# Trunk kernel on one core: block products of the feed-forward parts in strict order on TensorE, six matmuls per bank

## The chip, the cores and the metric

The kernel runs on one core of one Trainium2 chip. The metric is device time in microseconds, the median of several runs. Before the change it is 2380.13 us (3 runs, 2378.37 to 2385.53). All details below come from one profiled execution of that kernel, which took 2382.98 us. Engine names are those of the profile: PE is TensorE, PEld its weight loads, DVE VectorE, ACT ScalarE, POOL GpSimd, SP SyncE, which issues the transfers.

## The reference, cut to what matters

Two layers; each is a half-step feed-forward part, a mixing part, and another half-step feed-forward part. Sequence 512, model width 1024, hidden width 2816, everything in float32:

```python
def _swiglu(t, w_gate, w_up, w_down):
    return (jax.nn.silu(t @ w_gate) * (t @ w_up)) @ w_down
...
for l in range(DEPTH):
    f = _swiglu(_rmsnorm(h, ffn1_pre_g[l]), ffn1_w_gate[l], ffn1_w_up[l], ffn1_w_down[l])
    h = h + 0.5 * _rmsnorm(f, ffn1_post_g[l])
    ...  # three attention branches, gated, summed, projected
    f = _swiglu(_rmsnorm(h, ffn2_pre_g[l]), ffn2_w_gate[l], ffn2_w_up[l], ffn2_w_down[l])
    h = h + 0.5 * _rmsnorm(f, ffn2_post_g[l])
```

The change concerns the four feed-forward parts only. The kernel and the profile call them a0, c0 (layer 0), a1 and c1 (layer 1).

## The kernel before, in words

**A float32 product.** Each operand is split into a high part and a low part that TensorE takes at full rate. The split (`split`, L179) is one ScalarE copy for the high part (`wh`, L182) and one VectorE subtraction for the low part (`wl`, L183). One product of a 128-row tile is then three matmuls into the same PSUM bank, `mm3`: high by high (L205), high by low (L206), low by high (L207).

**Seven products for eight.** In a feed-forward part, most of the hidden width goes through a scheme of Strassen's kind: of a 2 by 2 product of blocks, seven block products are made instead of eight, of sums and differences of blocks. They are numbered 0 to 6 and run in the order 0, 2, 1, 3, 4, 5, 6. There are two column groups (0 and 1), and for each one a *gate* group and an *up* group of seven products (`token_product`, names `pw...g` and `pw...u`), then the *down* products of both (`product`, names `pd...`). Names carry the part: `pwc0g` is a gate product of c0, `pda` a down product of part a.

One product uses two PSUM banks, `pts[0]` and `pts[1]` (the loop variable `e`). Its weights come in two units of two 128-row tiles each (`k0` is 0 and 2, `kk` runs from 0 to 3). So it has 24 matmuls of 512 columns, 12 for each unit. Several products add into the same banks: products 0 and 2 open a pair, a copy of the first pair opens the third, and the table `SUM` says which product adds where. Product 6 uses the banks of product 5 and adds to the sum that stands in them; that sum has a use of its own and is read first. In the token groups that read is a VectorE addition, L777, one for each bank.

**Weights.** A unit's weights are loaded by SP (L297 for a block, 512 KB), combined with another block where the product needs that (VectorE, L327), and split (L182, L183). `wh` and `wl` are rings of four units. `Queue` (L350) emits a job's units, then those of the next jobs (four units ahead, `load_ahead`), and then the job's matmuls.

**Between the up group and the down products** the hidden values must be turned from one layout into the other. `turn`, called at two points of each unit, takes a finished part of the hidden values through a ScalarE copy (L800), a transpose by a transfer on SP (L801), and a ScalarE copy back (L804). The down products' first factors (`first_factor`) are made from these, with names `ah...` and `al...`.

**What sets the order.** The program emits instructions in the order of the jobs: all seven products of gate 0, of up 0, of gate 1, six of up 1, the first factor of the first down product, the last of up 1, and then the down products with plain gate and up tiles between them. A scheduler then orders the instructions of each engine by its own model; it may put a matmul that is ready by this model ahead of one that is emitted earlier. `tc.keep_in_program_order` ties an instruction to the one that stands before it on its engine in program order, so that the scheduler can't let it move. In the kernel before, the products' matmuls carry no such tie.

The loops that the change touches are those of `token_product` (from L740) and `product` (from L851), and `mm3` (L203).

Of the kernel before, what the change touches and what calls it, by code (L numbers as in the profile page):

```python
# [18 lines left out]
P = 128  # L19
# [4 lines left out]
def kernel(  # L24
# [38 lines left out]
    nc = tc.nc  # L63
# [4 lines left out]
    ND = D // P  # L68
# [7 lines left out]
    FC = 8  # L76
# [22 lines left out]
    def tmp(name):  # L99
        return sb.tile([P, S], F32, tag="f32t", bufs=5, name=name)  # L100
# [3 lines left out]
    def stile(shape, tag, name, dt=F32R):  # L104
        return sb.tile(shape, dt, tag=tag, bufs=BUFS[tag], name=name)
# [4 lines left out]
    def pbank(tag, name):  # L110
        return ps.tile([P, S], F32, tag=tag, bufs=4, name=name)
# [88 lines left out]
        nc.vector.scalar_tensor_tensor(t, z, minus, t, ALU.max, ALU.add)  # L200
        nc.scalar.activation(t, t, AF.Exp, scale=-1.0, bias=minus)

    def mm3(pt, lh, ll, rh, rl, start, stop, free=False):  # L203

        nc.tensor.matmul(pt, lh, rh, start=start, stop=False, skip_group_check=free)  # L205
        nc.tensor.matmul(pt, lh, rl, start=False, stop=False, skip_group_check=free)  # L206
        nc.tensor.matmul(pt, ll, rh, start=False, stop=stop, skip_group_check=free)  # L207

# [394 lines left out]
    def ffn(l, src, wg, wu, wd, dst, name, spare, parked, plan, aside=None):  # L603
# [12 lines left out]
        def hidden_rows(i):  # L616
            if i not in hr:
                hr[i] = stile([P, FC // 2, S], ("k", "tri")[i // 2], f"hr{name}_{i}", F32)
            return hr[i]
# [114 lines left out]
        def in_product(n):  # L734
            if n in (0, 1, 6):
                i, j = ((0, 0), (0, 1), None, None, None, None, (1, 1))[n]
                return [block(i, j, part) for part in range(2)]
            return st["u", n]

        def token_product(ci, up, n, uns):  # L740

            nm = f"{name}{'gu'[up]}_{ci}_{n}"
            if n in (0, 1, 2):
                st["c", n] = [pbank("z" if n == 0 else "mm", f"pw{nm}_{e}") for e in range(2)]
            if n == 1:
                for e in range(2):
                    nc.scalar.copy(st["c", 1][e][:], st["c", 0][e][:])
            if n == 0:
                if not up:
                    st["s", ci] = {}  # L750
            pts = st["c", SUM[n]]
            h, l = in_product(n)
            opens, ends = n in (0, 2), n in (1, 4, 6)
            for un in uns:
                for k in range(un.nk):
                    kk = un.k0 + k
                    for e in range(2):
                        c = slice(e * P, (e + 1) * P)
                        mm3(pts[e][:], h[:, kk, c], l[:, kk, c], un.h[:, k], un.l[:, k], opens and kk == 0,
                            ends and kk == ND // 2 - 1, free=True)  # L760
                        yield 3 * S * PE_US
                    turn(kk)
            if n == 0:
                return
            q = TO[n]
            g = st["s", ci]
            if not up and q not in g:
                g[q] = stile([P, FC // 2, S // 2], "f", f"s{name}_{ci}_{q[0]}{q[1]}", F32)[:]
            g = g[q]
            r = hidden_rows(2 * ci + q[1])[:, :, HALVES[q[0]]] if up else g  # L770
            for e in range(2):
                p = pts[e][:].rearrange("p (f q) -> p f q", f=2)
                re, ge = r[:, 2 * e:2 * e + 2], g[:, 2 * e:2 * e + 2]
                if n in (2, 3):
                    nc.scalar.copy(re, p)
                elif n in (4, 5):
                    nc.vector.tensor_tensor(re, re, p, ALU.add)  # L777
                elif up:
                    nc.vector.tensor_tensor(ge, p, ge, ALU.mult)
                else:  # L780
                    nc.scalar.activation(re, p, AF.Silu)
            if n in (4, 5):
                if up:
                    nc.vector.tensor_tensor(g, r, g, ALU.mult)
                else:
                    nc.scalar.activation(r, r, AF.Silu)
            if up and n in (1, 4, 5, 6):
                turns.append([nm, g, (2 * ci + q[1], q[0]), n in (1, 5), 0, None])

        def turn(kk):  # L790

            for one in turns:
                nm, g, (row, i), own, age, planes = one
                if kk == 1 and age == 0:
                    one[5] = planes = ([stile([P, 2, 2 * S], "rs", "tr" + nm, U16)[:, h] for h in range(2)] if own else
                                       [tmp(f"tr{nm}_{h}")[:].bitcast(U16) for h in range(2)])
                    words = g.rearrange("p f q -> p (f q)").bitcast(U16)
                    for h, plane in enumerate(planes):
                        part = tmp(f"th{nm}_{h}")[:].bitcast(U16)
                        nc.scalar.copy(part, words[:, h::2])  # L800
                        nc.sync.dma_start_transpose(plane.rearrange("p (r q) -> p r q", q=P), part)  # L801
                if kk in (0, 1) and age == 2:
                    r = hidden_rows(row)[:].bitcast(U16)
                    nc.scalar.copy(r[:, :, i * S + kk:(i + 1) * S:2].rearrange("p f (e q) -> p e f q", e=2),  # L804
                                   planes[kk].rearrange("p (e f q) -> p e f q", e=2, q=P))
                if kk == ND // 2 - 1:
                    one[4] += 1
            turns[:] = [one for one in turns if one[4] < 3]
# [20 lines left out]
        def first_factor(ci, n):  # L829

            a = lambda i, j: hr[2 * ci + j][:, :, HALVES[i]]
            nm = f"{name}_{ci}_{n}"
            h, l = (stile([P, FC // 2, S // 2], "v", f"a{x}{nm}")[:] for x in "hl")
            if n == 2:
                st["s", ci] = stile([P, FC // 2, S // 2], "v", f"as{nm}", F32)[:]
            s = st.get(("s", ci))
            if n == 2:
                nc.vector.tensor_tensor(s, a(1, 0), a(1, 1), ALU.add)
            elif n == 3:
                nc.vector.tensor_tensor(s, s, a(0, 0), ALU.subtract)  # L840
            elif n == 4:
                nc.vector.tensor_tensor(s, a(0, 1), s, ALU.subtract)
            elif n == 5:
                nc.vector.tensor_tensor(s, a(0, 0), a(1, 0), ALU.subtract)
            src = (a(0, 0), a(0, 1), s, s, s, s, a(1, 1))[n]
            split(h, l, src)
            st["a", ci, n] = h, l
# [3 lines left out]
        def product(at, uns):  # L851
            ci, n = DOWN[at]
            first, last = ci == 0, ci == NC - 1
            if at == 0:
                RINGS["o"] = 2
                dst.begin()
            if at + 1 < len(DOWN):
                first_factor(*DOWN[at + 1])
            if first and n in (0, 2):
                st["b", SUM[n]] = [pbank("z", f"pd{name}_{n}_{e}") for e in range(2)]  # L860
            pts = st["b", SUM[n]]
            h, l = st.pop(("a", ci, n))
            opens, ends = first and n in (0, 2), last and n in (1, 4, 6)
            for un in uns:
                for k in range(un.nk):
                    kk = un.k0 + k
                    for e in range(2):
                        c = slice(e * P, (e + 1) * P)
                        mm3(pts[e][:], h[:, kk, c], l[:, kk, c], un.h[:, k], un.l[:, k], opens and kk == 0,
                            ends and kk == FC // 2 - 1, free=True)  # L870
                        yield 3 * S * PE_US
                    turn(kk)
            if not last:
                return
            if n == 0:
                st["b", 1] = [pbank("z", f"pd{name}_1_{e}") for e in range(2)]
                for e in range(2):
                    nc.scalar.copy(st["b", 1][e][:], pts[e][:])
                return
            i, hf = TO[n]  # L880
            for e in range(2):
                f = dst.fs[2 * i + e][:, HF[hf]]
                if n in (4, 5):
                    nc.vector.tensor_tensor(f, f, pts[e][:], ALU.add)
                else:
                    nc.scalar.copy(f, pts[e][:])
# [817 lines left out]
```

## Time and profile before

| | us |
|---|---|
| median of 3 runs | 2380.13 |
| lowest, highest | 2378.37, 2385.53 |
| the profiled execution | 2382.98 |
| its span in the trace | 2380.9 |
| TensorE busy, matmuls | 2350.6 (11719) |
| VectorE busy | 1803.5 (2358 instructions) |
| ScalarE busy | 1513.8 (2306 instructions) |

The span is the time from the first to the last instruction in the trace; 2.1 us of the execution lie around it. A matmul in the profile shows about 0.39 us because matmuls are pipelined, while their starts show the pace. A row of a timeline has start, duration, engine, line, operation, the tile written and the tiles read (buffer numbers left out); in brackets stands how long the engine was idle ahead of it and what ended that. A row of a table of windows has the window, its length, busy time and number of instructions of PE, PEld, DVE, ACT and POOL, then the granted TensorE clock as a share of the full one, the share of time that the transfer engines were busy, and GB/s.

### The profile page before, as it was taken

How to read it: one execution, taken by the hardware profiler on the slowest of the kernel's cores; microseconds unless marked ns; L12 is line 12 of the kernel's file. 1: busy time of each engine (PE TensorE's matmuls, PEld its weight loads, DVE VectorE, ACT ScalarE, POOL GpSimd, SP SyncE). 2: the span in 40 equal slices, each digit the busy share in tenths (PEclk: the TensorE clock that was granted, in tenths of full speed). 3: DMA queues.
4: the chain of work that ended last, by engine and by line, in shares of the span. 5: the costliest groups of instructions: out<-in, count | busy, mean ns of one | idle time of the engine just before them, and what ended most of it. 6: DMA issues, size and time to landing. Idle time of an engine off the chain costs nothing.

```text
span 2380.9 us, 31151 instructions
## 1 busy us (share of the span) xinstructions
PE 2350.6 (99%) x11719; PEld 1984.2 (83%) x11719; DVE 1803.5 (76%) x2358; ACT 1513.8 (64%) x2306; POOL 75.8 (3%) x134
## 2 busy tenths in 40 slices
PE   9999999999999999999999999999999999999998
PEld 7787889888888888778888878889888888888787
DVE  8886877667777689778788778766767767888785
ACT  6777465577766556775656665655777665567744
POOL 0000000000111000000000000000001100000000
PEclk9999999999999999999999999999999999999999
DMA  5666455223223556664647664542323235566643
GB/s 197 195 174 174 161 196 151 71 80 94 87 78 103 189 179 182 170 195 135 236 128 200 186 185 153 192 124 71 94 76 98 73 123 193 161 204 174 197 143 141
DMA packets 299754, 354.98 MB, mean 149 GB/s; under 512 B 78266, under 2 KB 192978, under 8 KB 299604
## 3 DMA queue, kind: packets, MB, share of 16 engines
q1 hardware_dynamic: 299508, 352.97, 48.0%
q8 instruction: 92, 1.51, 0.3%
q14 instruction: 58, 0.48, 0.1%
q0 software_dynamic: 96, 0.03, 0.0%
HBM read 319.39 MB, written 16.78 MB: 141 GB/s over the span
## 4 chain that ended last, share of the span: by engine, by line
PE 85%; DVE 5%; DMA 4%; ACT 4%; issue 2%; SPq 0%; DVEq 0%; ACTq 0%
PE pg L206 4%; PE pg L205 4%; PE pg L207 4%; PE pdc L206 3%; PE pdc L207 3%; PE pdc L205 3%; PE pda L206 2%; PE pda L207 2%; PE pda L205 2%; PE pb L207 2%; PE pb L206 2%; PE pb L205 2%; PE pq L206 1%; PE pq L205 1%; PE pk L207 1%
## 5 line engine op out<-in xcount | busy, mean ns | idle before, releaser
L205 PE MATMUL pg<-us_a,wh_wg 128*128 128x512 f32 x384 | 151.0, 393 | 0.0
L207 PE MATMUL pg<-us_a,wl_wg 128*128 128x512 f32 x384 | 149.8, 390 | 0.0
L206 PE MATMUL pg<-us_a,wh_wg 128*128 128x512 f32 x384 | 149.8, 390 | 0.0
L206 PE MATMUL pdc<-wl_dc,ahc 128*128 128x512 f32 x224 | 87.9, 392 | 3.6 <-DVE wl_dc L183 3.6
L206 PE MATMUL pda<-wl_da,aha 128*128 128x512 f32 x224 | 87.9, 392 | 3.6 <-DVE wl_da L183 3.6
L205 PE MATMUL pda<-wh_da,aha 128*128 128x512 f32 x224 | 86.8, 390 | 2.0 <-ACT wh_da L182 2.0
L205 PE MATMUL pdc<-wh_dc,ahc 128*128 128x512 f32 x224 | 86.8, 390 | 0.6 <-ACT wh_dc L182 0.6
L207 PE MATMUL pda<-wh_da,ala 128*128 128x512 f32 x224 | 87.3, 390 | 0.0
L207 PE MATMUL pdc<-wh_dc,alc 128*128 128x512 f32 x224 | 87.2, 389 | 0.0
L183 DVE TENSOR_TENSOR wl_da<-raw_da,wh_da 128x1024 fp32r<-128x1024 f32 x50 | 60.9, 1224 | 34.3 <-ACT wh_da L182 34.3
L207 PEld LDWEIGHTS pg<-us_a,wl_wg 128*128 128x128 f32 x384 | 72.1, 188 | 15.2
L206 PEld LDWEIGHTS pg<-us_a,wh_wg 128*128 128x128 f32 x384 | 72.2, 188 | 14.1
L205 PEld LDWEIGHTS pg<-us_a,wh_wg 128*128 128x128 f32 x384 | 72.1, 188 | 14.1
L183 DVE TENSOR_TENSOR wl_dc<-raw_dc,wh_dc 128x1024 fp32r<-128x1024 f32 x50 | 61.0, 1223 | 29.0 <-ACT wh_dc L182 28.9
L182 ACT CAST wh_da<-raw_da 128x1024 fp32r<-128x1024 f32 x50 | 52.2, 1050 | 45.6 <-PE pda L207 15.3
L182 ACT CAST wh_dc<-raw_dc 128x1024 fp32r<-128x1024 f32 x50 | 52.3, 1049 | 42.7 <-PE pdc L207 18.0
L186 DVE SCALAR_TENSOR_TENSOR wl_wg<-raw_wg,wh_wg 128x1024 fp32r<-128x1024 f32 x48 | 58.4, 1221 | 22.3 <-ACT wh_wg L185 22.3
L200 DVE SCALAR_TENSOR_TENSOR ga<-pg,bgate,ga 128x512 f32<-128x512 f32 x48 | 35.9, 747 | 50.5 <-ACT ga L199 50.5
L185 ACT ACTIVATE wh_wg<-raw_wg 128x1024 fp32r<-128x1024 f32 x48 | 50.5, 1057 | 24.6 <-PE pv L1096 11.7
L183 DVE TENSOR_TENSOR wl_uc<-raw_uc,wh_uc 128x1024 fp32r<-128x1024 f32 x44 | 53.7, 1220 | 16.2 <-ACT wh_uc L182 16.2
L183 DVE TENSOR_TENSOR wl_ua<-raw_ua,wh_ua 128x1024 fp32r<-128x1024 f32 x44 | 53.6, 1220 | 16.0 <-ACT wh_ua L182 16.0
L182 ACT CAST wh_uc<-raw_uc 128x1024 fp32r<-128x1024 f32 x44 | 46.1, 1050 | 30.4 <-PE pgc L206 7.6
(647 smaller groups left out, 8057.6 us busy)
## 6 DMA issues: line engine op xcount, KB each, us to landing
raw_da<-in_ffn_w_down_dram SPq DMA_DIRECT2D x66, 512.0 KB, 4.5
raw_dc<-in_ffn_w_down_dram SPq DMA_DIRECT2D x66, 512.0 KB, 3.9
raw_ga<-in_ffn_w_gate_dram SPq DMA_DIRECT2D x52, 512.0 KB, 4.2
raw_ua<-in_ffn_w_up_dram SPq DMA_DIRECT2D x52, 512.0 KB, 4.5
raw_gc<-in_ffn_w_gate_dram SPq DMA_DIRECT2D x52, 512.0 KB, 3.9
raw_uc<-in_ffn_w_up_dram SPq DMA_DIRECT2D x52, 512.0 KB, 3.6
raw_wg<-in_w_gate_dram SPq DMA_DIRECT2D x48, 512.0 KB, 3.6
raw_wo<-in_w_out_dram SPq DMA_DIRECT2D x24, 512.0 KB, 3.3
```

Source lines behind the costliest of these rows:

```text
L182: both = [nc.scalar.copy(h_ap, src)]
L183: make = lambda: nc.vector.tensor_tensor(l_ap, src, h_ap.bitcast(F32), ALU.subtract)
L185: both = [nc.scalar.activation(h_ap, src, AF.Copy, scale=scale)]
L186: make = lambda: nc.vector.scalar_tensor_tensor(l_ap, src, scale, h_ap.bitcast(F32), ALU.mult, ALU.subtract)
L200: nc.vector.scalar_tensor_tensor(t, z, minus, t, ALU.max, ALU.add)
L205: nc.tensor.matmul(pt, lh, rh, start=start, stop=False, skip_group_check=free)
L206: nc.tensor.matmul(pt, lh, rl, start=False, stop=False, skip_group_check=free)
L207: nc.tensor.matmul(pt, ll, rh, start=False, stop=stop, skip_group_check=free)
```

## The change

In both loops the order of `k` (row tile in a unit) and `e` (bank) is exchanged. Before, each row tile had three matmuls into bank 0 and three into bank 1. After, a unit has six into bank 0 (both its row tiles) and then six into bank 1. `turn` is still called at two points of a unit, after six and after twelve matmuls. Besides, the first matmul into each bank of a product (`kk == 0`, for both `e`) is tied to its place in program order. The number of matmuls, their operands and the sum that each bank gets are the same.

```diff
-    def mm3(pt, lh, ll, rh, rl, start, stop, free=False):
-
-        nc.tensor.matmul(pt, lh, rh, start=start, stop=False, skip_group_check=free)
+    def mm3(pt, lh, ll, rh, rl, start, stop, free=False, pin=False):
+
+        one = nc.tensor.matmul(pt, lh, rh, start=start, stop=False, skip_group_check=free)
+        if pin:
+            tc.keep_in_program_order(one)
         nc.tensor.matmul(pt, lh, rl, start=False, stop=False, skip_group_check=free)
         nc.tensor.matmul(pt, ll, rh, start=False, stop=stop, skip_group_check=free)
...
             for un in uns:
-                for k in range(un.nk):
-                    kk = un.k0 + k
-                    for e in range(2):
-                        c = slice(e * P, (e + 1) * P)
+                for e in range(2):
+                    c = slice(e * P, (e + 1) * P)
+                    for k in range(un.nk):
+                        kk = un.k0 + k
                         mm3(pts[e][:], h[:, kk, c], l[:, kk, c], un.h[:, k], un.l[:, k], opens and kk == 0,
-                            ends and kk == ND // 2 - 1, free=True)
+                            ends and kk == ND // 2 - 1, True, kk == 0)
                         yield 3 * S * PE_US
-                    turn(kk)
+                    turn(un.k0 + e)
```

This is `token_product`; `product` has the same edit, with `FC` in place of `ND`. The changed kernel's lines stand two further down behind `mm3`.

More of the change, by code (lines that the diff above doesn't have):

```diff
@@ L864, in product @@
             for un in uns:
[L865 to L868, printed above, removed]
+                for e in range(2):
+                    c = slice(e * P, (e + 1) * P)
+                    for k in range(un.nk):
+                        kk = un.k0 + k
                         mm3(pts[e][:], h[:, kk, c], l[:, kk, c], un.h[:, k], un.l[:, k], opens and kk == 0,
-                            ends and kk == FC // 2 - 1, free=True)
+                            ends and kk == FC // 2 - 1, True, kk == 0)
                         yield 3 * S * PE_US
-                    turn(kk)
+                    turn(un.k0 + e)
             if not last:
```

## The prediction, made before the changed kernel was run

> **What bounds the kernel now.** I read the page first (span, busy shares, the chain that ended last), then TensorE's waits, then the timelines of TensorE, VectorE and ScalarE at the places that the diff touches.
>
> ```profile
> span 2380.9 us, 31151 instructions
> PE 2350.6 (99%) x11719; PEld 1984.2 (83%) x11719; DVE 1803.5 (76%) x2358; ACT 1513.8 (64%) x2306; POOL 75.8 (3%) x134
> PE 85%; DVE 5%; DMA 4%; ACT 4%; issue 2%; SPq 0%; DVEq 0%; ACTq 0%
> ```
>
> TensorE is busy for 99% of the span and holds 85% of the chain, so only idle TensorE time, or a stretch at a lower clock, can move the end. The number of matmuls doesn't change. The first question is whether the pattern of banks costs anything by itself.
>
> ```profile
> 905.45 0.39 PE L206 MATMUL pwc0g<-wl_gc,uhc 128*128 128x512 f32 x1
> 905.68 0.39 PE L207 MATMUL pwc0g<-wh_gc,ulc 128*128 128x512 f32 x1
> 905.90 0.39 PE L205 MATMUL pwc0g<-wh_gc,uhc 128*128 128x512 f32 x1
> 471.62 0.39 PE L206 MATMUL pb<-om,wh_wb 128*128 128x512 f32 x1
> 471.85 0.40 PE L207 MATMUL pb<-om,wl_wb 128*128 128x512 f32 x1
> ```
>
> The first column is the start. In a product (pwc0g: three matmuls into one bank, then the other; 905.68 to 905.90 crosses) starts stand 0.227 us apart; in pb, which stays in its bank, 0.23. So six in a row instead of three is worth nothing by itself, and all that is left is order: who is ahead of whom at the seams between groups.
>
> **The change part by part.** Product 6 ends a group and adds into the banks of product 5, so its first matmul into each bank waits until VectorE has read product 5's sum from there (L777). The order of instructions, built from both kernels, shows what program order takes away. Before, the scheduler let the first matmuls of the next group's product 0 stand ahead of product 6: 5 at gate to up of column group 0 (seam 1), 4 at up 0 to gate 1 (seam 2), 2 at gate 1 to up 1 (seam 3), 4 at up 1 to down (seam 4), in each of the four FFNs: 16 seams. After, all of product 6 comes first, six into bank 0 and then six into bank 1. On VectorE the two L777 stay behind the split of the next group's first weights (wl, L183) at seams 1, 3 and 4; at seam 2 the first of them moves ahead of it. So at three seams of four the filling goes and what it covered stays.
>
> *Seam 1*, as FFN c0 has it:
>
> ```profile
> 915.20 0.39 PE L207 MATMUL pwc0g<-wh_gc,ulc 128*128 128x512 f32 x1
> 915.42 0.61 PE L205 MATMUL pwc0u<-wh_uc,us_b 128*128 128x512 f32 x2
> 916.02 0.50 PE L206 MATMUL pwc0u<-wl_uc,us_b 128*128 128x512 f32 x1
> 916.83 0.40 PE L205 MATMUL pwc0g<-wh_gc,us_b 128*128 128x512 f32 x1
> 914.16 0.68 DVE L777 TENSOR_TENSOR sc<-sc,pwc0g 128x512 f32<-128x512 f32 x1
> 914.75 1.22 DVE L183 TENSOR_TENSOR wl_uc<-raw_uc,wh_uc 128x1024 fp32r<-128x1024 f32 x1
> 915.89 1.27 DVE L777 TENSOR_TENSOR sc<-sc,pwc0g 128x512 f32<-128x512 f32 x2
> ```
>
> Five up matmuls (pwc0u) run after product 5's last at 915.20, and product 6 starts at 916.83. After, it waits for the first L777: 915.89 + 0.68 (one L777, from the row at 914.16) = 916.57, + 0.06 until the matmul starts = 916.63. The second matmul after a restart comes about 0.10 late (seam 4 below: 195.69 to 196.02 is 0.33 for 0.227). It is thus 0.10 earlier than before in effect, and five matmuls (5 x 0.227 = 1.14) are still to be done: +1.0 us, +4.0 for four FFNs. The second L777 ends at 917.16, hidden behind the six matmuls into bank 0 (1.36 us); that is all that the six buy.
>
> *Seam 2*, FFN c0:
>
> ```profile
> 952.02 1.23 DVE L183 TENSOR_TENSOR wl_uc<-tuc,wh_uc 128x1024 fp32r<-128x1024 f32 x1 [0.53 <-ACT wh_uc L182]
> 953.60 0.39 PE L207 MATMUL pwc0u<-wh_uc,ulc 128*128 128x512 f32 x1
> 953.92 1.23 DVE L183 TENSOR_TENSOR wl_gc<-raw_gc,wh_gc 128x1024 fp32r<-128x1024 f32 x1 [0.67 <-ACT wh_gc L182]
> 955.07 1.28 DVE L777 TENSOR_TENSOR hrc<-hrc,pwc0u 128x512 f32<-128x512 f32 x2
> 956.00 0.39 PE L205 MATMUL pwc0u<-wh_uc,us_b 128*128 128x512 f32 x1
> ```
>
> Here VectorE stood idle for 0.67 ahead of wl_gc. After, the first L777 fits in there: 952.02 + 1.23 + 0.68 = 953.93, so product 6 starts at about 953.95. Then wl_gc takes until 955.16 and the second L777 until 955.84: matmul 7 starts at 955.9, with six done against four at 956.00. That is two matmuls and 0.10, less 0.10 for the restart: -0.45, and about -0.5 where the cast of wh_gc comes later. Four FFNs: -2.0.
>
> *Seam 3*, FFN c0:
>
> ```profile
> 992.98 0.39 PE L207 MATMUL pwc0g<-wh_gc,ulc 128*128 128x512 f32 x1
> 995.05 1.27 DVE L777 TENSOR_TENSOR sc<-sc,pwc0g 128x512 f32<-128x512 f32 x2
> 995.78 0.19 PEld L205 LDWEIGHTS pwc0g<-wh_gc,us_b 128*128 128x128 f32 x1 [0.41 <-DVE sc L777]
> 995.78 0.50 PE L205 MATMUL pwc0g<-wh_gc,us_b 128*128 128x512 f32 x1
> ```
>
> Product 6 starts right behind the first L777 already. After, it starts at the same time, with the two filling matmuls still to do: +0.45, +1.8 in all. TensorE is then idle for 995.78 - 993.37 = 2.4 us in one piece.
>
> *Seam 4*, FFN a0:
>
> ```profile
> 192.47 0.39 PE L207 MATMUL pwa0u<-wh_ua,ula 128*128 128x512 f32 x1
> 194.42 0.50 PE L205 MATMUL pda<-wh_da,aha 128*128 128x512 f32 x1 [1.57 <-ACT wh_da L182]
> 195.69 0.50 PE L206 MATMUL pda<-wl_da,aha 128*128 128x512 f32 x1 [0.76 <-DVE wl_da L183]
> 196.02 0.40 PE L207 MATMUL pda<-wh_da,ala 128*128 128x512 f32 x1
> 196.49 0.40 PE L205 MATMUL pwa0u<-wh_ua,us_x 128*128 128x512 f32 x1
> 195.55 1.28 DVE L777 TENSOR_TENSOR hra<-hra,pwa0u 128x512 f32<-128x512 f32 x2
> ```
>
> Product 6 starts after 195.55 + 0.68 + 0.06 = 196.29 instead of 196.49; with the restart's 0.10 that is 0.10 gained, and four matmuls (0.91) are left over: +0.8.
>
> What follows decides this seam, though. The up group's last products go through two transposes each (ACT copy L800, transpose L801, ACT copy back L804) while the down weights come in:
>
> ```profile
> 206.31 1.36 ACT L804 COPY hra<-tra0u 128x1024 uint16<-128x1024 uint16 x1
> 207.77 0.52 SPq L297 DMA_DIRECT2D raw_da<-in_ffn_w_down_dram  x1
> 214.57 0.37 SPq L297 DMA_DIRECT2D raw_da<-in_ffn_w_down_dram  x1
> 222.35 1.23 DVE L327 TENSOR_TENSOR bta<-bta,raw_da 128x1024 f32<-128x1024 f32 x1 [2.86 <-DMA raw_da<-in_ffn_w_down_dram]
> 224.77 0.50 PE L206 MATMUL pda<-wl_da,aha 128*128 128x512 f32 x1 [1.33 <-DVE wl_da L183]
> ```
>
> The load issued at 214.57 feeds the subtraction at 222.35, behind which VectorE's queue holds the split that TensorE waits for at 224.77. In the changed order ScalarE has one more copy back (1.36) ahead of that transpose's first copy, and SP has all three transposes ahead of the load that stood at 207.77 between them; the later load follows it, since it waits for the slot. I take both late by one copy, 1.4 us, which replaces the 0.8: TensorE would wait out the chain anyway. One matmul of the gate group now stands in that gap (-0.23). Seam 4: 1.4 - 0.23 = +1.17, +4.7 in all. Bounds: if the loads don't move, the wait at 224.77 swallows TensorE's 0.8 and the seam costs 0; if a load's issue (0.52) comes on top of the copy, 1.36 + 0.52 - 0.23 = +1.65, so 0 to +7 for four.
>
> Smaller swaps (a product 4 in FFN a0 whose two banks change places, a copy moved by one instruction near product 5, one load against one transpose) I set at nothing: each moves one or two matmuls of 0.227 either way, within 1 us, beside weights that are loaded ahead by four units.
>
> *The clock.* An edit that lengthens idle stretches may lower the granted clock.
>
> ```profile
> 106.00:126.00 20.00, 17.49 (x68) 13.71 (x68) 15.36 (x17) 16.09 (x17) 0.00 (x0) 0.91 0.84 207
> 194.00:222.00 28.00, 26.82 (x117) 21.95 (x118) 18.38 (x18) 24.81 (x26) 3.23 (x5) 1.00 0.81 216
> 994.00:1036.00 42.00, 40.79 (x169) 32.70 (x169) 31.21 (x30) 27.01 (x31) 0.00 (x0) 0.96 0.53 154
> 996.84 0.63 PE L205 MATMUL pwc0g<-wh_gc,us_b 128*128 128x512 f32 x1
> 997.27 0.63 PE L206 MATMUL pwc0g<-wl_gc,us_b 128*128 128x512 f32 x1
> ```
>
> The granted clock (third figure from the end) was 0.91 around a0's seam 2 and 0.96 behind c0's seam 3, where matmuls start 0.43 apart; (1 - 0.91) x 20 and (1 - 0.96) x 42 are 1.8 and 1.7 us. Around a0's seam 4, with idle pieces of 1.57 and 0.76, it was 1.00. So a drop follows some stalls and not others, and costs about 1.7. After, idle time at a seam is one piece: 2.4 at seam 3, 196.29 - 192.86 = 3.4 at a0's seam 4. I take no change (two drops remain somewhere); the bounds are both gone (-3.5) and four more (+7).
>
> [...]
>
> *Sum*: 4.0 - 2.0 + 1.8 + 4.7 + 0 = +8.5 us on the profiled execution, which took 2382.98 (span 2380.9, 2.1 outside). That is 0.12% above the median of the runs, 2380.13; the same +8.5 on the median gives 2388.6, **2389**.
>
> **The rivals.** (A) *The seams' idle time goes*: strict order ends the seams' stalls, as it would if VectorE read product 5's banks first. By the rows, TensorE's loss per FFN (time from product 5's last start to product 6's first, less 0.227 for each matmul) is 0.27 + 1.26 + 2.12 + 2.88 = 6.5 us, at most 26 for four: about 2355. For it: bank 0 of product 5 is finished six matmuls (1.36 us) earlier. Against: at seams 1, 3 and 4 L777 stands behind wl of the next group on VectorE, whose end doesn't move. It decides where L777 gets 1.2 us (one wl) earlier, to 914.75, 993.9 and 194.4, before product 5's last matmul has ended or soon after it.
> (B) *Waits only change places*: seam 2's gain, a lost clock drop and an unmoved load chain at seam 4 balance the rest: 4.0 - 2.0 + 1.8 + 0 - 3.5 = 0.3; 2375 to 2387. For it: the wait at 224.77 is there now and can absorb the seam.
> (C) *The clock*, on the slower side still: each unbroken idle piece above about 2 us (seams 3 and 4, eight of them) brings its own drop of 1.7. Six new ones: +8.5 + 10 = 2399. It decides from idle pieces of 2 us. For it: the pieces are broken by filling matmuls now. Against: 1.00 around a0's seam 4.
> (D) *The pattern of banks itself*: at 0.227 against 0.23 it gives nothing, in either direction; a variant of B.
>
> **How the numbers follow.** A change under 0.3% (7 us) can't be told from none here. Forecast (2383 to 2394) 0.47; B 0.28; C 0.12; A 0.13. Faster by over 0.3% (below 2373): A and a rest of B, 0.14. Within: most of B and the low end of the forecast, 0.31. Slower: 0.55. The range takes in the forecast, B and C with the bounds above (-3 - 2 and +20): 2375 to 2401, and leaves out A.
>
> **What would show it.** In the changed profile TensorE should show, at seams 1, 3 and 4, one idle piece ahead of product 6's first L205, ended by VectorE's L777, of about 1.0, 2.4 and 3.4 us (c0, c0, a0); at seam 2 a short one, and a second ended by L777 in the middle of product 6. VectorE's L777 should start behind wl of the next group. The wait for wl_da L183 at 224.77 should be there and later by one to two us, with the load before it issued later. 0.227 between matmuls elsewhere. The forecast is wrong if L777 runs ahead of that wl at seams 1, 3 or 4, if the two loads of the down weights don't move, or if the stretches of 0.43 spacing multiply.

## The result, and the profile after

The changed kernel takes 2398.6 us (median of 4 runs, 2394.35 to 2404.38) against 2379.77 before: ratio 1.0078, 95% interval 1.0058 to 1.0098. A second set (`after_rep` below) gave 1.0081 (1.0062 to 1.0101). It is slower, by about 19 us; the prediction said 2389, range 2375 to 2401. The profiled execution is the fastest of the four, 2394.35, 11.4 above the one of before. That spread matters below.

The page of the changed kernel, with the lines shown of before (matmuls of `mm3` are now L205, L208, L209; L777 is L779, other lines stand two down):

```profile
span 2392.6 us, 31177 instructions
PE 2348.3 (98%) x11719; PEld 1985.3 (83%) x11719; DVE 1804.8 (75%) x2358; ACT 1514.9 (63%) x2306; POOL 75.5 (3%) x134
PE 85%; DVE 7%; DMA 3%; ACT 3%; issue 2%; SPq 0%; POOL 0%; DVEq 0%; ACTq 0%
```

As many matmuls, TensorE's busy time 2 us shorter, the span 11.7 longer: what came is idle time. VectorE's share of the chain rose from 5% to 7%. TensorE's waits say where (us in total, times, longest):

```profile
PE pwc0u L205 <- ACT ahc L182: 3.4, 1, 3.4
PE pwc1g L205 <- DVE sc L779: 3.3, 2, 2.2
PE pwa0g L205 <- DVE sa L779: 3.0, 2, 2.6
PE pwa1g L205 <- DVE sa L779: 2.9, 2, 1.7
PE pdc L208 <- DVE wl_dc L183: 2.8, 2, 1.7
PE pwa0u L205 <- ACT aha L182: 2.7, 1, 2.7
```

The list before was led by waits for weights (wh, wl); now the first matmul of product 6 waits for L779 (the rows that name ahc and aha are taken up below). Seam 1 of c0, TensorE's rows and then VectorE's:

```profile
917.94 0.39 PE L209 MATMUL pwc0g<-wh_gc,ulc 128*128 128x512 f32 x1
919.46 0.47 PE L205 MATMUL pwc0g<-wh_gc,us_b 128*128 128x512 f32 x1 [1.13 <-DVE sc L779]
917.50 1.21 DVE L183 TENSOR_TENSOR wl_uc<-raw_uc,wh_uc 128x1024 fp32r<-128x1024 f32 x1
918.64 1.27 DVE L779 TENSOR_TENSOR sc<-sc,pwc0g 128x512 f32<-128x512 f32 x2
```

Product 5 ends, VectorE first makes wl_uc, which only the next group needs, then reads product 5's bank, and TensorE stands still for 1.13 us. Seam 4 of a0 (TensorE, VectorE, ScalarE):

```profile
195.43 0.39 PE L209 MATMUL pwa0u<-wh_ua,ula 128*128 128x512 f32 x1
198.53 0.47 PE L205 MATMUL pwa0u<-wh_ua,us_x 128*128 128x512 f32 x1 [2.70 <-ACT aha L182]
196.56 1.23 DVE L183 TENSOR_TENSOR wl_da<-raw_da,wh_da 128x1024 fp32r<-128x1024 f32 x1
197.70 1.28 DVE L779 TENSOR_TENSOR hra<-hra,pwa0u 128x512 f32<-128x512 f32 x2
197.38 1.04 ACT L182 CAST aha<-hra 128x1024 fp32r<-128x1024 f32 x1
```

The view names ScalarE's aha as what ended the wait, but aha is no operand of this matmul. The first L779 ends at 197.70 + 0.68 = 198.38 (0.68 is one L779 of the pair) and the matmul starts 0.15 later, just as at seam 1 (918.64 + 0.68 = 919.32, then 919.46); at each of the 13 seams where product 6 starts late in this profile, it starts 0.14 or 0.15 us after the end of an L779. The cast ends at about the same time, 198.42. That product 6 doesn't wait for it is seen in a kernel of the last experiment below, `e9_defer`, where the reads come first: there product 6 of a0 starts before this cast does.

```profile
192.04 0.39 PE L205 MATMUL pwa0u<-wh_ua,us_x 128*128 128x512 f32 x1
192.44 1.05 ACT L182 CAST aha<-hra 128x1024 fp32r<-128x1024 f32 x1
```

Summing, over all matmuls of the block products, the time by which one start follows the other later than 0.227 us gives the table (all four feed-forward parts, us). Outside the kernel's first 12 us, starts 0.427 apart count as half clock, 0.2 each, together with the slower starts at both ends of such a stretch:

| where | before | after | difference | forecast |
|---|---|---|---|---|
| seam 1 | 0.8 | 4.8 | +4.0 | +4.0 |
| seam 2 | 6.3 | 3.7 | -2.6 | -2.0 |
| seam 3 | 5.6 | 9.0 | +3.4 | +1.8 |
| seam 4 | 7.8 | 11.6 | +3.8 | +4.7 with the next line |
| wait for wl_da, wl_dc behind it | 5.3 | 6.5 | +1.2 | |
| stretches at half clock | 3.2 (2) | 4.7 (3) | +1.5 | 0 |

### The profile page after: what moved, and what is told of

The parts are those of the page before. It is cut to its first block, busy times and chain, and to the rows that moved or that the text cites. A ratio compares the mean times of both kernels' runs of the same rounds, so it can differ in the third digit from the quotient of the medians.

```text
span 2392.6 us, 31177 instructions
## 1 busy us (share of the span) xinstructions
PE 2348.3 (98%) x11719; PEld 1985.3 (83%) x11719; DVE 1804.8 (75%) x2358; ACT 1514.9 (63%) x2306; POOL 75.5 (3%) x134
## 4 chain that ended last, share of the span: by engine, by line
PE 85%; DVE 7%; DMA 3%; ACT 3%; issue 2%; SPq 0%; POOL 0%; DVEq 0%; ACTq 0%
PE pg L208 4%; PE pg L209 4%; PE pg L205 4%; PE pda L208 3%; PE pda L209 3%; PE pda L205 3%; PE pdc L208 2%; PE pdc L209 2%; PE pdc L205 2%; PE pb L209 2%; PE pb L208 2%; PE pb L205 2%; PE pq L208 1%; PE pq L205 1%; PE pk L208 1%
## 5 line engine op out<-in xcount | busy, mean ns | idle before, releaser
L205 PE MATMUL pg<-us_a,wh_wg 128*128 128x512 f32 x384 | 150.9, 393 | 0.0
L209 PE MATMUL pg<-us_a,wl_wg 128*128 128x512 f32 x384 | 149.8, 390 | 0.0
L208 PE MATMUL pg<-us_a,wh_wg 128*128 128x512 f32 x384 | 149.8, 390 | 0.0
L208 PE MATMUL pdc<-wl_dc,ahc 128*128 128x512 f32 x224 | 87.6, 391 | 2.8 <-DVE wl_dc L183 2.8
L208 PE MATMUL pda<-wl_da,aha 128*128 128x512 f32 x224 | 87.6, 391 | 2.6 <-DVE wl_da L183 2.6
L209 PE MATMUL pdc<-wh_dc,alc 128*128 128x512 f32 x224 | 87.2, 389 | 0.0
L209 PE MATMUL pda<-wh_da,ala 128*128 128x512 f32 x224 | 87.2, 389 | 0.0
L205 PE MATMUL pda<-wh_da,aha 128*128 128x512 f32 x224 | 86.9, 389 | 0.0
L205 PE MATMUL pdc<-wh_dc,ahc 128*128 128x512 f32 x224 | 86.8, 389 | 0.0
L209 PEld LDWEIGHTS pg<-us_a,wl_wg 128*128 128x128 f32 x384 | 72.1, 188 | 15.2
L208 PEld LDWEIGHTS pg<-us_a,wh_wg 128*128 128x128 f32 x384 | 72.2, 188 | 14.1
L205 PEld LDWEIGHTS pg<-us_a,wh_wg 128*128 128x128 f32 x384 | 72.1, 188 | 14.1
L185 ACT ACTIVATE wh_wg<-raw_wg 128x1024 fp32r<-128x1024 f32 x48 | 50.6, 1058 | 25.0 <-PE pv L1098 11.7
```

The costliest lines, as they stand in the source:

```text
L185: both = [nc.scalar.activation(h_ap, src, AF.Copy, scale=scale)]
L205: one = nc.tensor.matmul(pt, lh, rh, start=start, stop=False, skip_group_check=free)
```

## The experiments

The theory is that product 6 waits for VectorE to read product 5's banks; the matmuls that ran ahead covered this wait, and strict order takes the cover away. Its rivals are that the pattern of six matmuls per bank costs the time, that the clock does, or that waits only change places, so that no edit at the seams moves the end. All ratios are to the kernel before, run on the same chip. "Waits" is the sum of the table's method without the half-clock part: 30 us for before, 42 for the changed kernel.

### The loops alone, and the tie alone

```diff
-                            ends and kk == ND // 2 - 1, True, kk == 0)
+                            ends and kk == ND // 2 - 1, True)
```

> The loops exchanged (six matmuls per bank), no matmul tied to its place. The scheduler again lets 5, 2 and 4 matmuls of the next group run ahead of product 6 at seams 1, 3 and 4; at seam 2 it lets none, and the first read L779 stands ahead of the next weights' split there, as in the changed kernel. Theory (the cost is the reads of product 5's banks, no longer covered by filling matmuls): seams 1, 3 and 4 cost what they cost before (about 0.3, 1.6 and 1.9 us each), seam 2 gains about 0.8 each, so about 2377 to 2382, within 0.2% of before. Rival (six matmuls in a row into one bank are slow by themselves): as slow as the changed kernel, about 2398. Rival (the clock falls more often for some other reason): between the two, with a mean granted clock of 0.995.

Measured: 2382.4 us, ratio 0.9998 (0.9987 to 1.0010), waits 29. Six per bank cost nothing: that rival falls.

The other half, `pin` in the kernel before with its loops as they were:

```diff
-                            ends and kk == ND // 2 - 1, free=True)
+                            ends and kk == ND // 2 - 1, True, kk == 0)
```

> The tie alone: matmuls alternate three per bank as before, and product 6 stands in program order. VectorE has both reads behind the next weights' split at all four seams. Theory: the four seams cost as in the changed kernel or more, since at seam 2 the first read no longer moves ahead of the split (about 2 us per seam there against 0.9): 2398 to 2406. Rival (the pattern of banks costs the time): back at about 2380. If the tie costs and the six per bank give something back, this kernel is slower than the changed one by 4 to 8 us.

Measured: 2410.76 us, ratio 1.0116 (1.0099 to 1.0132), waits 49. The tie is the cost. The changed loops give part of it back (the intervals of 1.0116 and of the changed kernel's 1.0081, from two chips, just touch, so the size is rough). Seam 2 shows how (c0, the tie alone, VectorE and then TensorE):

```profile
962.81 1.23 DVE L183 TENSOR_TENSOR wl_gc<-raw_gc,wh_gc 128x1024 fp32r<-128x1024 f32 x1 [0.67 <-ACT wh_gc L182]
963.95 1.28 DVE L779 TENSOR_TENSOR hrc<-hrc,pwc0u 128x512 f32<-128x512 f32 x2
964.78 0.46 PE L205 MATMUL pwc0u<-wh_uc,us_b 128*128 128x512 f32 x1 [1.81 <-ACT wh_gc L182]
```

and the changed kernel at the same place:

```profile
956.74 0.68 DVE L779 TENSOR_TENSOR hrc<-hrc,pwc0u 128x512 f32<-128x512 f32 x1
957.49 1.23 DVE L183 TENSOR_TENSOR wl_gc<-raw_gc,wh_gc 128x1024 fp32r<-128x1024 f32 x1
958.63 0.68 DVE L779 TENSOR_TENSOR hrc<-hrc,pwc0u 128x512 f32<-128x512 f32 x1
959.37 0.50 PE L205 MATMUL pwc0u<-wh_uc,us_b 128*128 128x512 f32 x1 [0.16 <-DVE hrc L779]
```

With six per bank, bank 0 is finished earlier and the scheduler put its read ahead of wl_gc; TensorE waits 0.16 for the second read, in the middle of product 6, instead of 1.81 ahead of it.

### The tie in the token products only

```diff
-                            ends and kk == FC // 2 - 1, True, kk == 0)
+                            ends and kk == FC // 2 - 1, True)
```

> The changed kernel with the tie in the token products only, not in the down products: at seam 4 four down matmuls run ahead of product 6 again, seams 1 to 3 stay strict. By the two profiles seam 4 costs 3.0, 2.3, 2.6 and 2.6 us in the changed kernel without its clock drop against 2.9, 1.7, 1.7 and 1.5 before, and the wait for the split of the down weights behind it 1.6 against 1.3 on the mean. Theory: this goes back, 3 to 5 us, and a drop of the clock or two with it: 2391 to 2396. Rival (seam 4 costs nothing, since the load chain behind it sets the time): within 1.5 us of the changed kernel.

Measured: 2389.8 us, ratio 1.0029 (1.0017 to 1.0042), waits 39 us. So the tie at seam 4 does cost time. The gain over the changed kernel (1.0081) is some 12 us, more than the 3 to 5 expected. The waits give 3. The mean granted clock of its runs was 0.9968 against 0.9951 in ten runs of the changed kernel, and 0.0017 x 2390 is another 4. The rest, 5 us, stays open.

### The changed kernel again, and its idle time filled

> The changed kernel once more, without an edit, so that the others can be set against it, and to see how its times spread. If lower clock in the unbroken idle pieces makes the spread, its executions lie further apart than those of the kernel before, and the slower ones show the lower mean granted clock; the profile should again lose about 29 us at the 16 seams plus 1.4 to 1.7 for each stretch of 0.43 spacing.

Measured: 2402.74 us (6 runs, 2398.16 to 2408.54), ratio 1.0081. Its profile is of the slowest execution: waits 46 us, and eight stretches at half clock (65 starts, 13 us) against three (21 starts, 4 us) in the first profile. So executions of one kernel differ by how many stretches they have. One begins right behind seam 4 of c0 (first profile):

```profile
1039.49 0.47 PE L205 MATMUL pwc0u<-wh_uc,us_b 128*128 128x512 f32 x1 [3.37 <-ACT ahc L182]
1039.80 0.50 PE L208 MATMUL pwc0u<-wl_uc,us_b 128*128 128x512 f32 x1
1040.10 0.63 PE L209 MATMUL pwc0u<-wh_uc,us_b 128*128 128x512 f32 x1
1040.53 0.63 PE L205 MATMUL pwc0u<-wh_uc,us_b 128*128 128x512 f32 x1
```

Idle for 3.37 us, then starts 0.43 apart until 1043.45. The windows at four seams of the second profile (third figure from the end: granted clock):

```profile
1040.00:1052.00 12.00, 8.45 (x26) 6.42 (x25) 8.50 (x9) 9.92 (x11) 0.00 (x0) 0.72 0.40 88
1388.00:1398.00 10.00, 7.70 (x28) 5.85 (x27) 7.68 (x9) 8.83 (x10) 0.00 (x0) 0.83 0.48 106
2190.00:2204.00 14.00, 11.12 (x37) 8.59 (x37) 7.96 (x10) 6.34 (x7) 0.00 (x0) 0.76 0.58 184
2234.00:2244.00 10.00, 7.29 (x27) 5.61 (x26) 7.94 (x8) 8.93 (x10) 0.00 (x0) 0.83 0.46 105
```

The test is to fill the idle time and leave the waits:

```diff
+            if n == 6:
+                st["z"] = [pbank("z", f"pn{nm}_{e}") for e in range(2)]
+                for j in range({(0, 0): 4, (1, 0): 0, (0, 1): 8, (1, 1): 8}[up, ci]):
+                    tc.keep_in_program_order(nc.tensor.matmul(st["z"][0][:], h[:, 0, 0:P], uns[0].h[:, 0], start=True, stop=False, skip_group_check=True))
...
```

The next product 0 takes over the bank and overwrites it.

> The changed kernel with idle time filled by matmuls that nobody needs: ahead of product 6, 4 at seam 1, 8 at seams 3 and 4 (0.9 and 1.8 us), into the bank that the next product 0 opens and overwrites. They take none of the waits away. Theory (the clock falls in unbroken idle pieces): the waits for the reads end when they ended before, the stretches of 0.43 spacing at the seams become rare, and the time falls by 4 to 10 us from the changed kernel's 1.0080 of the kernel before, to a ratio of about 1.004 to 1.006. Rival (clock drops don't follow the idle pieces): the ratio stays at 1.007 or above, or rises where the filling is longer than the wait.

Measured: 2397.41 us (5 runs), ratio 1.0054 (1.0042 to 1.0067), with 80 matmuls more. In its profile, at seams 3 and 4 of c0 and seam 4 of a1 and c1:

```profile
994.00:1004.00 10.00, 10.00 (x45) 8.28 (x45) 6.26 (x7) 5.76 (x7) 0.00 (x0) 1.00 0.69 213
1034.00:1044.00 10.00, 9.89 (x44) 7.87 (x43) 9.00 (x10) 10.00 (x11) 0.00 (x0) 1.00 0.46 106
1378.00:1388.00 10.00, 9.74 (x44) 7.74 (x43) 9.07 (x10) 10.00 (x11) 0.00 (x0) 1.00 0.50 107
2223.00:2233.00 10.00, 9.70 (x43) 7.70 (x43) 9.02 (x11) 10.00 (x11) 0.00 (x0) 1.00 0.47 107
```

The granted clock is 1.00 at all of them. Two stretches were left, one at seam 2 of a0 (no filling there) and one at the wait for wl_dc behind seam 4 of c0. The mean granted clock of its runs is 0.9972. The delay of product 6 stayed in sum: from product 5's last start to product 6's first, less 0.227, the 16 seams come to 26.1 us, against 26.7 and 28.0 in the two profiles of the changed kernel, though it moved between seams (2.3 to 4.5 in all at seam 2, 11.3 to 8.7 at seam 4). So useless work in the idle pieces saved about 0.27%, some 6 us: that much of the slowdown was clock. The two intervals (1.0042 to 1.0067, 1.0062 to 1.0101, on two chips) overlap at the edge, so the size is rough; the sign is also what the windows show.

### The reads first

If the theory holds, putting the reads ahead of the next group's weights removes the seams' waits. First by splitting fewer units ahead at product 5, and tying the splits made at product 6:

```diff
+                    n = getattr(units[0], "n", None) if units and units[0].name[0] in "gu" else None
+                    self.pinned = n == 6
                     if not self.hold:
-                        self.load_ahead()
+                        self.load_ahead(2 if n == 5 else self.AHEAD)
+                    self.pinned = False
```

> The changed kernel, but a token group's product 5 splits only two units ahead, and the splits emitted at product 6 are tied to their place: on VectorE the reads of product 5's banks (L779, here L782) stand ahead of the next group's first weights at seams 1, 2 and 3, and at seam 4 the first of the two does. TensorE's order stays strict. Theory: bank 0 is finished six matmuls (1.36 us) before product 5 ends and its read takes 0.68, so product 6 starts at once at all seams and the four seams' loss goes (about 29 of 46 us in the changed kernel's profile): 2366 to 2376, faster than before. Rival (product 6 waits for its own weights or for a transfer): within 4 us of the changed kernel. Rival (the later split of the next group's weights makes product 0 late by as much): 2390 to 2398.

Measured: 2383.62 us, ratio 1.0000 (0.9992 to 1.0009), waits 33. Seams 1 to 3 lost 0 to 0.3 us each as expected, but the time was 8 to 18 us above the forecast: at seam 4 the first factor's split still stood ahead of the read (0.9 to 2.0 us each), and the tied splits of product 2 came late (1.6 us at three places). A second form mended both: only the next group's first two units tied, and the first factor's split behind the reads.

```diff
+                    if n == 6:
+                        self.pinned = True
+                        self.load_ahead(2)
+                        self.pinned = False
...
+                def a_job():
+                    Q.pinned = True
+                    first_factor(n, 0)
+                    Q.pinned = False
+                    return iter(())
```

> The changed kernel with the reads first at all four seams: product 5 (and the job of the first factor ahead of the last up product) splits only two units ahead; at product 6 only the next group's first two units are tied behind the reads, later ones are free; the first factor's split is tied behind the reads too. Against the earlier form (e3_read) the reads now lead at seam 4 as well, and the second units of product 2 aren't held back. Theory: product 6 starts within 0.3 us of product 5's end at all 16 seams; of e3_read's 35 us of lost time about 8 at seam 4 and 5 to 7 at product 2 go: 2368 to 2376. Rival (TensorE waits for the loads of the down weights whatever the seams do): what is saved at seam 4 comes back at the wait for wl_da and wl_dc, 2376 to 2384.

Measured: 2385.84 us, ratio 1.0008 (0.9996 to 1.0020). The rival had the mechanism, though the time is 2 us above its range. The longest of its waits:

```profile
PE pdc L208 <- DVE wl_dc L183: 6.2, 2, 3.7
PE pda L208 <- DVE wl_da L183: 4.7, 2, 2.5
...
PE pwc0g L205 <- ACT pwc0g L756: 1.7, 1, 1.7
```

The wait for the down weights is 10.9 us instead of 5.4 (2.8 and 2.6) in the changed kernel. Seam 4 won 9 us (11.3 to 2.3 ahead of product 6 in the four parts), and 5.5 of them come back there: the awaited split ends 30.9 us behind product 6's start on the mean, against 29.7 in the changed kernel's first profile. That this is because weights split later free their slots later is argued, not shown. TensorE also waits for the copy L756 at the start of product 1, 3.6 us in all (1.7 the longest). The clock was low as well: 0.9955 on the mean of its runs against 0.9978 in the kernel before beside them, by estimate 5 us.

The same edit in the kernel before:

> The same reads first in the kernel before: no tie on TensorE, three matmuls per bank. With bank 0 read early the scheduler finds product 6 ready and lets almost nothing run ahead of it. Theory (the place of the reads decides, neither the tie nor the six per bank): within 4 us of e7_read2, a little slower where the second read ends later than three matmuls cover. Rival (strict order or six per bank is worth something by itself once the reads lead): 5 us or more slower than e7_read2.

Measured: 2382.59 us, ratio 0.9998 (0.9986 to 1.0009). It is 3 us below the last: strict order shows no worth by itself.

The third form leaves the casts where they are and puts off only the low parts (wl) of the next two units, until the reads are emitted; the first factor's split is tied as in the second form:

```diff
-            self.split_from(src)
-            self.loaded()
+            if Q.defer is None or self.n:
+                self.split_from(src)
+                self.loaded()
+                return
+            make = self.split_from(src, later=True)
+            Q.defer.append(lambda: (tc.keep_in_program_order(make()), self.loaded()))
...
+            if n == 5:
+                late, Q.defer = Q.defer, None
+                for one in late:
+                    one()
```

> The changed kernel with one thing moved: the casts of the next group's first two units stay where they are, and only their low parts (wl) are put off until product 5's two reads are emitted, and tied behind them, at all four seams; the first factor's split is tied behind the reads at seam 4. TensorE's order is that of the changed kernel. Theory: the 16 seams' waits (29 us of the changed kernel's 42 us of lost time without clock drops) go, and little comes back at seams 1 to 3. At seam 4 the slots of the down weights come free 2.5 us later than in the changed kernel, not 5.4 as in e7_read2, so the wait for wl_da and wl_dc behind it takes about 2 us each instead of 1.3 to 2: 2372 to 2380. Rival (every gain at a seam returns at the next wait, since ScalarE and VectorE set the pace): 2382 to 2388, as for e7_read2.

Measured: 2376.2 us, ratio 0.9969 (0.9958 to 0.9979), waits 22. The rival falls, and this version beats both kernels. Run again:

> e9_defer once more, to compare with e13_defer_before on the same chip and to see that its gain holds: ratio 0.996 to 0.998.

it gave 2377.11 us, 0.9968 (0.9958 to 0.9979). In the first of the two profiles (span 2372.3 us), seam 1 of c0 and the two largest waits are:

```profile
912.32 0.39 PE L209 MATMUL pwc0g<-wh_gc,ulc 128*128 128x512 f32 x1
912.70 0.47 PE L205 MATMUL pwc0g<-wh_gc,us_b 128*128 128x512 f32 x1
911.27 1.28 DVE L786 TENSOR_TENSOR sc<-sc,pwc0g 128x512 f32<-128x512 f32 x2
912.74 0.69 DVE L786 TENSOR_TENSOR sc<-sc,pwc0g 128x512 f32<-128x512 f32 x1 [0.19 <-PE pwc0g L209]
913.35 2.35 DVE L183 TENSOR_TENSOR wl_uc<-raw_uc,wh_uc 128x1024 fp32r<-128x1024 f32 x2
```

```profile
PE pdc L208 <- DVE wl_dc L183: 3.0, 2, 1.5
PE pda L208 <- DVE wl_da L183: 3.0, 2, 1.9
```

The first read of product 5's banks is the second of the pair at 911.27, the other follows at 912.74, wl_uc comes last, and product 6 starts 0.38 us behind product 5's last start instead of 1.52. The wait for the down weights is 6.0. In the profile of the second set (span 2378.5) it is 8.8, and all waits together are 28.

The same with seam 4 left as in the kernel before (no low part put off at up 1, and no tie in the down products):

```diff
+                    ... and units[0].name[:1] + units[0].name[-5:-4] != "u1":
+                        self.defer = []
```

> The low parts put off behind the reads at seams 1 to 3 only, and the tie on TensorE in the token products only: at seam 4 four down matmuls run ahead of product 6 as in the kernel before, and its loads stay where they are. Theory: seams 1 to 3 cost about 0.2 us each (2.2, 4.7 and 4.2 us in all in the kernel before, without clock drops, are 11), seam 4 and the wait behind it stay (13 us): 2368 to 2376, ratio 0.994 to 0.997, the fastest of all. Rival (each gain returns at the next wait): 2380 to 2386, ratio 0.999 to 1.001.

Measured: 2378.66 us, ratio 0.9978 (0.9969 to 0.9987), waits 26. Faster than before, but short of the forecast (0.994 to 0.997): 4 of the 12 seams 1 to 3 still waited 1.2 to 2.1 us. And the low parts put off in the kernel before, without any of the change:

> The kernel before (three matmuls per bank, no tie) with the same low parts put off behind the reads. The scheduler now lets only one or two matmuls ahead of product 6 in the first part's groups and next to none elsewhere. Theory (the place of the reads is the whole gain): within 3 us of e9_defer, ratio 0.996 to 0.999, a little slower where the second read ends later than three matmuls cover (0.2 to 0.4 us at a seam, up to 5 us in all). Rival (once the reads lead, six matmuls per bank in strict order are needed for the gain): ratio 0.999 or above.

Measured: 2376.18 us, ratio 0.9976 (0.9965 to 0.9986), against 0.9968 for the version with the change on the same chip. The two can't be told apart: the intervals overlap, and the medians (2376.18 and 2377.11) lie the other way round. The place of the reads is the gain; no run shows that six per bank and the tie add to it.

## Why the prediction was right and where it was not

The forecast was slower by 9 us, in a range that holds the 2398.6; it was right in sign and cause, and less than half the size: 8.5 us forecast, 18.8 measured.

- **Bank pattern at nothing**: right. The loops alone gave 0.9998.
- **Seam 1, +1.0 each**: right; 1.13 us idle at c0 for a forecast of 1.0, and +4.0 in all.
- **Seam 2, -2.0**: right, -2.6. The idle stood in the middle of product 6, and the first L779 ahead of wl_gc, as forecast. At a0 product 6 still started 2.3 us late, behind a late cast (wh_ga).
- **Seam 3, +1.8**: too small, +3.4. c0, from which it was worked out, even gained (1.42 us idle for a forecast of 2.4), while a0 lost 2.7: it went from almost no loss to 2.6 us idle. One seam stood for four that differ. At a0 the delay comes from a product earlier: VectorE reads product 4's banks at 152.16 instead of 149.39, behind them in turn stand ScalarE's L788 and its cast of wh_ua, then wl_ua on VectorE, and then product 5's reads, at 156.63 instead of 154.16. What made product 4's reads late stays open.
- **Seam 4 and the load chain, +4.7**: the sum is right (+5.0), but partly by luck. The prediction let the later loads replace the seam's own 0.8; in the runs the seam cost 0.95 in each part (+3.8) and the wait behind it 0.3 more (+1.2). The later load is there:

```profile
206.68 4.74 SPq L803 DMA_TRANSPOSE tra0u<-tha0u  x3
211.51 0.53 SPq L299 DMA_DIRECT2D raw_da<-in_ffn_w_down_dram  x1
225.11 1.23 DVE L329 TENSOR_TENSOR bta<-bta,raw_da 128x1024 f32<-128x1024 f32 x1 [1.42 <-DMA raw_da<-in_ffn_w_down_dram]
227.53 0.50 PE L208 MATMUL pda<-wl_da,aha 128*128 128x512 f32 x1 [1.08 <-DVE wl_da L183]
```

  All three transposes stand ahead of the load, issued at 211.51 instead of 207.77: 3.7 later, of which product 6's own shift (196.49 to 198.53) is 2.0, so 1.7 for a forecast of 1.4.
- **The clock, "I take no change"**: this step failed. The first profile shows only one stretch more, but the median does not follow that execution. The mean granted clock was 0.9951 over ten runs of the changed kernel and 0.9978 over 23 of the kernel before beside six of them: 0.0027 x 2390 = 6 us. The filled kernel gives the same size by another way. Rival C had the mechanism. Its total (2399) agrees partly by luck, with 10 us of clock where the means give 6, and its rule doesn't hold: idle pieces of 2.63 and 2.70 us in the first profile brought no drop, while one of 1.81 in the kernel with the tie alone, which ended at 964.78, was followed by a drop at 965.59. So the length of a piece doesn't decide by itself; what else does, these runs don't show. Here are two windows of 3.41 us, as long as a stretch, around the piece of 2.70 in the changed kernel (seam 4 of a0; it ends at 198.53), and then one ahead of the drop and one in it at seam 2 of c0 with the tie alone:

```profile
193.44:196.85 3.41, 2.38 (x11) 1.65 (x9) 3.41 (x4) 3.41 (x5) 0.00 (x0) 1.00 0.03 10
196.85:200.26 3.41, 1.73 (x8) 1.47 (x9) 3.41 (x5) 3.41 (x4) 0.00 (x0) 1.00 0.89 158
```

```profile
962.17:965.59 3.42, 1.61 (x8) 1.05 (x7) 2.78 (x4) 3.17 (x4) 0.00 (x0) 1.00 0.72 110
965.59:969.00 3.41, 3.41 (x10) 2.65 (x9) 1.91 (x2) 1.04 (x2) 0.00 (x0) 0.50 1.09 308
```

  The granted clock was 1.00 in both windows around the piece of 2.70, and 0.50 for the 3.41 us from 965.59. TensorE was busy for 1.61 us in the window ahead of that drop, and for 2.38 and 1.73 in the two without one; two cases give no rule. The stretch behind seam 4 of c0 is as long: a granted clock of 0.50 from 1039.94 to 1043.35. The changed kernel's two profiles have 3 and 8 stretches where the one of before has 2, so one to six more: by estimate 1.6 to 9.6 us at 1.6 each (the table has 3.2 for two and 4.7 for three), and the 6 us of the means lie between.
- **Rival A**, the seams' idle time goes: not by this change, but it named the point where it would, reads one wl earlier. The version that puts them there has 22 and 28 us of waits in its two profiles, against 42 and 46.
- **Rival B**, waits only change places: wrong for the change, right in part for the second form of the reads first, where 5.5 us came back.

The terms measured add up: 4.0 - 2.6 + 3.4 + 5.0 = 9.8 of waits, 6 of clock on the mean of the runs, and 3 that the table doesn't place. The changed kernel's second profile has 4 us more of waits than the first, so the 3 lie within what its executions differ by.

## What to carry to other kernels

When an order on one engine is made strict, ask what the matmuls that ran ahead were covering; here it was a read of a bank, queued on another engine behind work that was not yet due. Move that read first: putting off two subtractions by a microsecond or two gained 0.3%, where ordering TensorE lost 0.8%. Put off as little as possible: the form that put off the casts as well lost at the next wait more than half of what it had won at seam 4. And price idle pieces of about two microseconds and more above their length: with the tie alone one of 1.81 us was followed by 3.41 us at half clock, though those of 2.63 and 2.70 in the changed kernel were not.

## What the runs showed of the hardware that was not expected

The number of half-clock stretches differs between executions of one kernel, 3 and 8 in two profiles of the changed kernel (2394.35 and 2408.54 us). The length of an idle piece doesn't tell whether one follows: none did behind pieces of 2.63 and 2.70 us in the first of these profiles, one did behind 1.81 us with the tie alone. The two in the kernel before and the three in that first profile last 3.41 us each at a granted clock of 0.50, and cost about 1.6 us (eight slower starts, 0.427 instead of 0.227 apart at most). Two of the eight in the second profile last about 6.7, by mean granted clocks of 0.72 over 12 us and 0.76 over 14. TensorE restarted 0.14 to 0.15 us after the end of VectorE's read at 13 seams of the changed kernel, where 0.06 was taken.
